# Strassen's seven products for the up and gate projections, and w2 in four parts

## The chip, the cores and the metric

The kernel runs on one core of one Trainium2 chip. Five engines work side by side, each with its own queue of instructions, and wait for each other through semaphores: TensorE (PE; its weight loads are shown apart as PEld), VectorE (DVE), ScalarE (ACT), GpSimd (POOL) and SyncE (SP, which only issues transfers). The metric is the device time of one execution in microseconds (us). One execution before was also recorded by the hardware profiler; its rows are what follows is read from.

## The reference

The model is a trunk of two layers over 512 tokens of width 1024. Each layer is a feed-forward sublayer (FFN), a mixer of three branches, and a second FFN; every sublayer is modulated by a conditioning vector and closed by a layer norm. All is float32. The FFN is what the change touches:

```
def swiglu(h, w1, w3, w2):
    return (jax.nn.silu(h @ w1) * (h @ w3)) @ w2

f = swiglu(modulate(h, shift, scale), w1, w3, w2)     # w1, w3: 1024 x 2816, w2: 2816 x 1024
h = layer_norm(alpha * h + 0.5 * gate * f)
```

There are four FFNs, (0, 0), (0, 2), (1, 0) and (1, 2) as (layer, place); the mixers are (0, 1) and (1, 1).

## The kernel before

Activations lie transposed: x is 8 tiles, one for each 128 of the width, with 512 tokens in the columns. A float32 product is made of three passes (mm3, line 126): the weight and the activation are each split into a high part, rounded to the format that TensorE multiplies, and a low part, the rest; the passes are high with high, high with low, and low with high. `split` (line 132) makes both parts of an activation: the high one by ACT (line 135), the low one by DVE (line 138).

Weights come in chunks of four 128x128 tiles, 128x512 in all. `wtile` (lines 99 to 117) issues the transfer on SP, has ACT round the high part (line 109, tile whi) and DVE subtract it from the raw chunk (line 111, tile wlo). In tails, where `share` is set, POOL subtracts every other one. There are 9 buffers of whi and wlo (WBUFS).

`gemm` (line 539) multiplies a column of weight tiles with x into one PSUM bank of 512 columns and then calls `tick`, which lets one step of side work run: the conditioning's matrix (`ada_jobs`, line 207, two DVE reductions on a transferred chunk for each 128 outputs, line 185), and, under the first FFN of a layer, the tables and state-space powers of the coming mixer (lines 480 to 760; the powers are the short POOL operations of lines 529 to 537).

An FFN (`ffn_body`, line 442) goes over 22 column blocks f of 128. The first ones are made by `first_block` (line 397), three in the first FFN and two in the others, there in two halves of 256 tokens, with the steps of the previous sublayer's norm between their matmuls. For every f follow a gemm with w1, a gemm with w3, and `swiglu_out` (line 430): silu on ACT, the product on DVE, the split into the tile pair g. After 11 blocks their g is multiplied by the upper half of w2 and added, times the gate G, to the residual H (lines 470 to 473); G must be ready by then (line 468). The other 11 go through `tail` (line 372): as each of the 8 column blocks of w2 is done, the sums of the norm are formed; the last three blocks are done in halves of 256 tokens, and `norm` (line 319) of the first half runs beside the matmuls of the second. `norm` spreads mean and deviation over the partitions by a matmul (line 316), subtracts, scales, modulates (lines 345 to 364) and last scales H for the next residual on POOL (line 368).

The order of the work is that of the program, as the framework's scheduler issues it: each engine takes its instructions strictly in the order printed, and one that waits holds up those behind it.

Of the kernel before, what the change touches and what calls it, by code (L numbers as in the profile page):

```python
# [9 lines left out]
F32 = mybir.dt.float32  # L10
# [6 lines left out]
P = 128  # L17
# [18 lines left out]
WBUFS, RBUFS, ABUFS = 9, 4, 2  # L36
# [4 lines left out]
class Packer:  # L41


    def __init__(self):
        self.tiles = []
        self.ada = []


class Builder:
    def __init__(self, nc, tc, ctx, A, pk, plan):  # L50
# [11 lines left out]
        self.ntile = 0  # L62
        self.nada = 0
        self.cur = None
        self.share = False
# [33 lines left out]
    def wtile(self, key):  # L99

        i = self.ntile % CH
        if i == 0:
            nc = self.nc
            c = self.ntile // CH
            raw = self.wp.tile([P, CH * P], F32, tag="wraw", name=f"wraw{c}", bufs=RBUFS)
            nc.sync.dma_start(raw, self.A["ws"][c])
            hi = self.wp.tile([P, CH * P], F32R, tag="whi", name=f"whi{c}", bufs=WBUFS)
            lo = self.wp.tile([P, CH * P], F32R, tag="wlo", name=f"wlo{c}", bufs=WBUFS)
            nc.scalar.copy(hi, raw)  # L109
            e = nc.gpsimd if self.share and c % 2 else nc.vector  # L110
            e.tensor_tensor(lo, raw, hi.bitcast(F32), ALU.subtract)  # L111
            self.cur = (hi, lo)
        self.ntile += 1
        self.pk.tiles.append(key)
        hi, lo = self.cur
        s = slice(i * P, (i + 1) * P)
        return hi[:, s], lo[:, s]

    def wide(self, keys):

        assert self.ntile % CH == 0 and len(keys) == CH
        for key in keys:
            self.wtile(key)
        return self.cur
# [247 lines left out]
    def tail(self, keys, xs, G, nxt, last):  # L372
# [3 lines left out]
        NS = 4 if len(xs) == KT else 3  # L376
# [53 lines left out]
    def swiglu_out(self, f, g, p1, p3, a, b):  # L430
        nc = self.nc
        n = b - a
        s = self.t(self.fp, "sil", 3)
        nc.scalar.activation(s[:, :n], p1, AF.Silu)
        nc.vector.tensor_tensor(s[:, :n], s[:, :n], p3, ALU.mult)  # L435
        self.normed = self.split(s[:, :n], g[0][:, a:b], g[1][:, a:b]).ins

# [4 lines left out]
    def ffn_body(self, l, i, nxt, last, pend):  # L442
        fi = 0 if i == 0 else 1
        G = self.mod[l, i][2]
        NH = DFF // P // 2
        for hf in range(2):
            f0 = hf * NH
            g = []
            ahead = []
            if hf == 0:  # L450
                fs = range(2 if pend else 3)
                g = [self.pair(self.fp, "g", 12) for _ in fs]
                names = [lambda k, f=f, m=m: (m, (l, fi), k, f) for f in fs for m in ("ffn_w1", "ffn_w3")]
                if pend is None:
                    names.append(lambda k: ("ffn_w1", (l, fi), k, 3))
                for a, b, pp in self.first_block(names, pend):
                    ahead = pp[2 * len(fs):]
                    for f in fs:
                        self.swiglu_out(f, g[f], pp[2 * f], pp[2 * f + 1], a, b)
            for f in range(f0 + len(g), f0 + NH):  # L460
                pp, ahead = ahead, []
                for m in ("ffn_w1", "ffn_w3")[len(pp):]:
                    pp.append(self.gemm([(m, (l, fi), k, f) for k in range(KT)], self.x))
                gt = self.pair(self.fp, "g", 12)
                self.swiglu_out(f, gt, pp[0], pp[1], 0, S)
                g.append(gt)
            if hf == 0:
                while (l, i) not in self.gated:
                    self.tick()
# [1017 lines left out]
```

## Time and profile before

| | |
|---|---|
| three runs | 2890.91, 2893.56, 2895.76 us, median 2893.56 us |
| profiled execution | 2893.78 us, span of the instructions 2891.7 us |
| mean granted TensorE clock | 0.987 |
| PE busy | 2801.3 us, 14360 matmuls |
| DVE busy | 1646.4 us, 4266 instructions |
| ACT busy | 1111.9 us, 2174 instructions |
| POOL busy | 438.7 us, 685 instructions |
| chunks of weights | 916, of them 872 low parts on DVE and 44 on POOL |

Engines overlap, so their busy times don't add up. The busy time of PE is that of overlapping, pipelined matmuls; the distance from one start to the next is what one of them costs. Lines such as L111 are the kernel's lines. Names such as wlo<-wraw,whi say what was written from what.

### The profile page before, as it was taken

The page shows a single profiled execution, that of the slowest core. Times are in us where ns is not written, and L with a number is a line of the kernel's source. Part 1 is how long each engine was busy: PE and PEld are TensorE (multiplying, and loading weights), DVE is VectorE, ACT ScalarE, POOL GpSimd, SP SyncE. Part 2 cuts the span into 40 slices and gives each one's busy share as a digit, 9 for nine tenths or more (in the row PEclk, how much of TensorE's full clock was granted, in tenths as well). Part 3 has the DMA queues.
Part 4 walks back from the last instruction along what each step waited for, and adds up shares of the span by engine and source line. Part 5 has one row for each costly group of instructions (what it writes and reads, how often), then busy time and mean ns, then how long its engine had stood idle before and what let it go on. Part 6 is the DMA issues. An engine that isn't in the chain of part 4 may idle for free.

```text
span 2891.7 us, 40692 instructions
## 1 busy us (share of the span) xinstructions
PE 2801.3 (97%) x14360; PEld 2364.6 (82%) x14360; DVE 1646.4 (57%) x4266; ACT 1111.9 (38%) x2174; POOL 438.7 (15%) x685
## 2 busy tenths in 40 slices
PE   8999998999999999999999999989999999999997
PEld 6888886978888888888888888869788888888886
DVE  8755459983444465544476454699734444653334
ACT  4333344373443344223343233543643433432332
POOL 2120365000000050000411003730000000500004
PEclk9999999999999999999999999999999999999998
DMA  7545345543233324544344453446422333253331
GB/s 279 167 136 146 113 125 155 182 135 117 85 90 113 98 67 146 153 124 142 88 123 143 131 148 97 149 146 190 146 81 84 99 110 98 70 150 102 95 99 51
DMA packets 205836, 359.38 MB, mean 124 GB/s; under 512 B 23104, under 2 KB 40000, under 8 KB 205632
## 3 DMA queue, kind: packets, MB, share of 16 engines
q1 hardware_dynamic: 198864, 346.32, 40.2%
q10 hardware_dynamic: 6768, 10.47, 1.1%
q8 instruction: 112, 1.84, 0.3%
q14 instruction: 92, 0.75, 0.1%
HBM read 339.92 MB, written 16.78 MB: 123 GB/s over the span
## 4 chain that ended last, share of the span: by engine, by line
PE 82%; DVE 7%; POOL 5%; ACT 3%; DMA 2%; issue 1%; ACTq 0%; SPq 0%; DVEq 0%; POOLq 0%
PE ps L128 26%; PE ps L129 25%; PE ps L130 25%; DMA wraw<-ws 1%; PE ps L894 1%; DMA araw<-wa 1%; DVE wlo L111 1%; POOL half L533 1%; POOL half L536 1%; ACT whi L109 1%; PE ps L316 1%; PE ps L1085 1%; DVE araw L185 1%; PE ps L997 1%; PE ps L1074 0%
## 5 line engine op out<-in xcount | busy, mean ns | idle before, releaser
L109 ACT CAST whi<-wraw 128x512 fp32r<-128x512 f32 x916 | 564.7, 621 | 1320.6 <-PE ps L129 931.4
L111 DVE TENSOR_TENSOR wlo<-wraw,whi 128x512 fp32r<-128x512 f32 x872 | 609.8, 703 | 740.8 <-ACT whi L109 723.2
L128 PE MATMUL ps<-xh,whi 128*128 128x512 f32 (+1 forms) x2496 | 938.7, 379 | 15.4 <-ACT xh L135 15.4
L129 PE MATMUL ps<-xl,whi 128*128 128x512 f32 (+1 forms) x2496 | 941.4, 378 | 0.2 <-DVE xl L138 0.2
L130 PE MATMUL ps<-xh,wlo 128*128 128x512 f32 (+1 forms) x2496 | 939.5, 377 | 0.0
L128 PEld LDWEIGHTS ps<-xh,whi 128*128 128x128 f32 x2496 | 469.5, 189 | 103.0 <-ACT xh L135 18.4
L129 PEld LDWEIGHTS ps<-xl,whi 128*128 128x128 f32 x2496 | 471.1, 189 | 85.3 <-issue 1.2
L130 PEld LDWEIGHTS ps<-xh,wlo 128*128 128x128 f32 x2496 | 471.0, 189 | 85.4 <-issue 0.5
L128 PE MATMUL ps<-gh,whi 128*128 128x512 f32 (+1 forms) x836 | 303.8, 363 | 0.2 <-ACT gh L135 0.2
L129 PE MATMUL ps<-gl,whi 128*128 128x512 f32 (+1 forms) x836 | 299.4, 358 | 0.2 <-DVE gl L138 0.2
L130 PE MATMUL ps<-gh,wlo 128*128 128x512 f32 (+1 forms) x836 | 299.2, 358 | 0.0
L111 POOL TENSOR_TENSOR wlo<-wraw,whi 128x512 fp32r<-128x512 f32 x44 | 57.5, 1307 | 1159.7 <-ACT whi L109 1159.7
L128 PEld LDWEIGHTS ps<-gh,whi 128*128 128x128 f32 x836 | 160.4, 192 | 25.5 <-issue 2.5
L129 PEld LDWEIGHTS ps<-gl,whi 128*128 128x128 f32 x836 | 160.3, 192 | 25.3 <-issue 2.5
L130 PEld LDWEIGHTS ps<-gh,wlo 128*128 128x128 f32 x836 | 160.1, 191 | 22.3
L303 POOL TENSOR_TENSOR H<-H,ln 128x512 f32<-128x512 f32 x6 | 7.8, 1293 | 968.3 <-ACT ln L302 968.3
L435 DVE TENSOR_TENSOR sil<-sil,ps 128x512 f32<-128x512 f32 (+1 forms) x94 | 61.1, 652 | 117.3 <-PE ps L130 113.6
L185 DVE CUSTOM_DVE_ANT_0 araw<-araw,cond,cols 128x512 f32<-128x512 f32 x128 | 96.7, 755 | 14.8 <-DMA araw<-wa 14.8
L185 DVE CUSTOM_DVE_ANT_0 araw<-araw,cond,adac 128x512 f32<-128x512 f32 x128 | 96.2, 751 | 10.9 <-DMA araw<-wa 9.9
L286 DVE SCALAR_TENSOR_TENSOR H<-ps,G,H 128x256 f32<-128x256 f32 (+1 forms) x68 | 40.2, 592 | 82.5 <-PE ps L130 82.4
L128 PE MATMUL ps<-whi,xh 128*128 128x512 f32 x192 | 80.8, 423 | 1.3 <-DVE vst L949 1.2
L130 PE MATMUL ps<-whi,xl 128*128 128x512 f32 x192 | 77.9, 406 | 0.0
(518 smaller groups left out, 3555.3 us busy)
## 6 DMA issues: line engine op xcount, KB each, us to landing
wraw<-ws SPq DMA_DIRECT2D x916, 256.0 KB, 2.7
araw<-wa SPq DMA_DIRECT2D x256, 256.0 KB, 2.8
raw<-wa SPq DMA_DIRECT2D x16, 512.0 KB, 6.9
vd<-vst SPq DMA_DIRECT2D x24, 256.0 KB, 2.1
V<-vd SPq DMA_DIRECT2D x24, 256.0 KB, 5.5
hd<-H SPq DMA_DIRECT2D x32, 128.0 KB, 1.8
H<-hd ACTq DMA_DIRECT2D x16, 256.0 KB, 3.2
H<-xT SPq DMA_DIRECT2D x8, 256.0 KB, 7.6
```

The source lines that it names most:

```text
L109: nc.scalar.copy(hi, raw)
L111: e.tensor_tensor(lo, raw, hi.bitcast(F32), ALU.subtract)
L128: nc.tensor.matmul(ps, w[0], x[0], start=start, stop=False)
L129: nc.tensor.matmul(ps, w[0], x[1], start=False, stop=False)
L130: nc.tensor.matmul(ps, w[1], x[0], start=False, stop=stop)
L185: self.nc.vector.tensor_tensor_reduce(out=w, in0=w, in1=self.cond[:, k0:k0 + n], scale=1.0, scalar=a if k0 else self.col(("b_ada", l), q), ...
L286: nc.vector.scalar_tensor_tensor(h, ps, G[:, j:j + 1], h, ALU.mult, ALU.add)
L316: self.nc.tensor.matmul(ps, self.ones, dg, start=True, stop=True)
L435: nc.vector.tensor_tensor(s[:, :n], s[:, :n], p3, ALU.mult)
L533: tt(t, a[1], b[1], ALU.mult)
L536: tt(t, a[1], b[0], ALU.mult)
L894: nc.tensor.matmul(s, q[:, P * i:P * i + P], K[:, :w], start=True, stop=True)
```

## The change

In the products with w1 and w3, x, W and the result are taken as two by two blocks: the rows of the result are the two halves of the tokens, the inner dimension is split into even and odd 128-tiles, and the column blocks are f and f + 1. Strassen's scheme in Winograd's form makes the four blocks of the result from seven block products instead of eight, with sums of blocks of x and of W as operands. A "group" is two column blocks of w1 and of w3 together: w1's block and w3's block stand side by side, so that 7 products of 24 matmuls with 256 columns replace 96 matmuls with 512 columns.

`combine_x` forms the combinations of x once for each FFN: POOL adds high and low parts of the 8 tiles, DVE makes four combinations and three splits for each pair of tiles. `group` forms those of W by 8 POOL subtractions of raw chunks (held in 12 buffers, sraw), calls `parts` for 14 chunks, combines the seven products by 7 DVE additions, and makes g by silu on ACT, 2 multiplications on POOL and the two parts (ACT and DVE). The products with w2 go in four parts of 6, 6, 4 and 6 column blocks: the first three are added to H, the last is the tail, whose last four blocks are always done in halves. There are 8 buffers of whi and wlo. The gates' conditioning is computed one sublayer earlier, but for the first FFN, where eight steps of side work run after each group until the gate is ready. No side work runs inside a group; two steps run in each gemm with w2.

```diff
-WBUFS, RBUFS, ABUFS = 9, 4, 2
+WBUFS, RBUFS, ABUFS = 8, 4, 2
+PARTS = (6, 6, 4, 6)
+SBUFS = 12
...
+    def parts(self, raw, pool=False):
+        nc = self.nc
+        hi = self.wp.tile([P, CH * P], F32R, tag="whi", name=self.name("whi"), bufs=WBUFS)
+        lo = self.wp.tile([P, CH * P], F32R, tag="wlo", name=self.name("wlo"), bufs=WBUFS)
+        nc.scalar.copy(hi, raw)
+        e = nc.gpsimd if pool else nc.vector
+        e.tensor_tensor(lo, raw, hi.bitcast(F32), ALU.subtract)
+        return hi, lo
...
-        NS = 4 if len(xs) == KT else 3
+        NS = 4
...
+    def combine_x(self):
...
+            for t, x in ((t0, x0), (t1, x1)):
+                nc.gpsimd.tensor_tensor(t, x[0].bitcast(F32), x[1].bitcast(F32), ALU.add)
+            d = nc.vector
+            a11, a21, a12, a22 = t0[:, :H], t0[:, H:], t1[:, :H], t1[:, H:]
+            d.tensor_tensor(a22, a21, a22, ALU.add)
+            d.tensor_tensor(a21, a11, a21, ALU.subtract)
+            d.tensor_tensor(a11, a22, a11, ALU.subtract)
+            d.tensor_tensor(a12, a12, a11, ALU.subtract)
+            s41 = self.pair(self.fp, "s41", KT // 2)
+            s2 = [self.t(self.fp, z, KT // 2, H, F32R) for z in ("s2h", "s2l")]
+            self.split(a11, *s2)
+            self.split(t1, *s41)
+            self.split(a21, x0[0][:, H:], x0[1][:, H:])
...
+    def group(self, l, fi, f, B, g, after):
...
+        def product(x, w):
+            ps = self.pst()
+            for d in range(2):
+                hi, lo = self.parts(w[d])
+                for q in range(2):
+                    for s in range(2):
+                        o = P * (2 * q + s)
+                        self.mm3(ps[:, H * s:H * s + H], (hi[:, o:o + P], lo[:, o:o + P]), self.xs[2 * d + q][x],
+                                 d + q + s == 0, d + q + s == 3)
+            return ps
...
+        p1 = product("A11", B["11"])
+        for d in range(2):
+            sub(B["11"][d], B["12"][d], B["11"][d])
+        for d in range(2):
+            sub(T2[d], B["22"][d], B["11"][d])
+        nc.scalar.copy(r0, p1)
+        self.group_load(l, fi, after, N, "11")
+        p2 = product("A12", B["21"])
+        for d in range(2):
+            sub(B["12"][d], B["22"][d], B["12"][d])
+        for d in range(2):
+            sub(B["21"][d], B["21"][d], T2[d])
+        add(r1, r0, p2)
+        nc.scalar.activation(r1, r1, AF.Silu)
...
+        add(r2, r0, product("S2", T2))
+        p5 = product("S1", B["11"])
...
+        add(r3, r2, product("S3", B["12"]))
+        add(r2, r2, p5)
+        add(r0, r3, p5)
+        add(r2, r2, product("S4", B["22"]))
+        nc.gpsimd.tensor_tensor(r2, r2, r1, ALU.mult)
+        out(r2, 0)
+        p4 = product("A22", B["21"])
...
+        add(r3, r3, p4)
+        nc.scalar.activation(r3, r3, AF.Silu)
+        nc.gpsimd.tensor_tensor(r0, r0, r3, ALU.mult)
+        out(r0, 1)
...
-                for n in range(KT):
-                    ps = self.gemm([("ffn_w2", (l, fi), f0 + k, n) for k in range(NH)], g)
-                    h = self.H[n]
-                    self.nc.vector.scalar_tensor_tensor(h, ps, G[:, n:n + 1], h, ALU.mult, ALU.add)
+        self.combine_x()
+        f0 = 0
+        for n in PARTS:
+            while f < f0 + n:
+                B = self.group(l, fi, f, B, g, f + 2 if f + 2 < DFF // P else None)
+                f += 2
+                if (l, i) not in self.gated:
+                    self.tick(8)
+            if f == DFF // P:
+                break
+            while (l, i) not in self.gated:
+                self.tick()
+            for j in range(KT):
+                ps = self.gemm([("ffn_w2", (l, fi), f0 + k, j) for k in range(n)], g)
+                self.tick()
+                h = self.H[j]
+                self.nc.vector.scalar_tensor_tensor(h, ps, G[:, j:j + 1], h, ALU.mult, ALU.add)
+            f0, g = f, []
...
-                yield from self.ada_jobs(l, i, True)
+                if first:
+                    yield from self.ada_jobs(l, i, True)
                 if nxt is not None:
                     yield from self.ada_jobs(*nxt, False)
+                    yield from self.ada_jobs(*nxt, True)
```

Two places of the order are shown. The first is DVE in FFN (0, 2), where the second half of x has just been normed. Before, the last low parts of x (xl, line 138) are mixed with those of the next gemms' weights (wlo, line 111):

```order
1776 L138 TENSOR_TENSOR xl_9700<-half_10441,xh_9699 128x256
1777 L138 TENSOR_TENSOR gl_10268<-sil_10505,gh_10267 128x256
1778 L111 TENSOR_TENSOR wlo_10642<-wraw_10639,whi_10641 128x512
1779 L138 TENSOR_TENSOR xl_9702<-half_10447,xh_9701 128x256
1780 L138 TENSOR_TENSOR xl_9704<-half_10452,xh_9703 128x256
1781 L111 TENSOR_TENSOR wlo_10663<-wraw_10660,whi_10662 128x512
1782 L111 TENSOR_TENSOR wlo_10681<-wraw_10678,whi_10680 128x512
```

In the changed kernel the same engine goes from the combinations of x (lines 476 to 479, on the tiles ln and lndg that POOL's sums fill; line 152 is `split`) to the weights of the first group (line 130, from sraw):

```order
1992 L476 TENSOR_TENSOR lndg_11871<-ln_1947_11870,lndg_11871 128x256
1993 L152 TENSOR_TENSOR s41l_11861<-ln_1942_11853,s41h_11860 128x512
1994 L477 TENSOR_TENSOR ln_1947_11870<-ln_1947_11870 128x256
1995 L130 TENSOR_TENSOR wlo_11898<-sraw_11800,whi_11897 128x512
1996 L478 TENSOR_TENSOR ln_1947_11870<-lndg_11871,ln_1947_11870 128x256
1997 L152 TENSOR_TENSOR xl_10884<-ln_1947_11870,xh_10883 128x256
1998 L479 TENSOR_TENSOR lndg_11871<-lndg_11871,ln_1947_11870 128x256
1999 L152 TENSOR_TENSOR s2l_11881<-ln_1947_11870,s2h_11880 128x256
2000 L130 TENSOR_TENSOR wlo_11914<-sraw_11802,whi_11913 128x512
2001 L152 TENSOR_TENSOR s41l_11879<-lndg_11871,s41h_11878 128x512
2002 L130 TENSOR_TENSOR wlo_11940<-sraw_11804,whi_11939 128x512
```

The first low part of weights, row 1995, stands behind row 1992, which reads the last of the eight sums (lndg_11871), and the second one, row 2000, behind five more operations on that pair. On POOL the same place reads so: the last steps of the norm (line 382, L368 before), the sums (line 473), and behind them the first group's subtractions (line 527):

```order
422 L382 TENSOR_SCALAR H_10860<-H_10860,R_94 128x256
423 L382 TENSOR_SCALAR H_10861<-H_10861,R_94 128x256
424 L382 TENSOR_SCALAR H_10862<-H_10862,R_94 128x256
425 L473 TENSOR_TENSOR ln_1941_11852<-xh_10879,xl_10880 128x512
426 L473 TENSOR_TENSOR ln_1942_11853<-xh_10881,xl_10882 128x512
427 L473 TENSOR_TENSOR ln_1947_11870<-xh_10883,xl_10884 128x512
428 L473 TENSOR_TENSOR lndg_11871<-xh_10885,xl_10886 128x512
429 L527 TENSOR_TENSOR sraw_11800<-sraw_11808,sraw_11800 128x512
430 L527 TENSOR_TENSOR sq_11890<-sraw_11812,sraw_11800 128x512
431 L527 TENSOR_TENSOR sraw_11808<-sraw_11812,sraw_11808 128x512
```

Before, nothing of this FFN's matmuls came from POOL at this place; now row 428 is ahead of DVE's row 1992, and rows 429 and 430 ahead of the operands of the products S1 and S2. The second place is POOL in the first FFN, at the end of the state-space powers (lines 532 to 537). Before, the powers are followed by the tail's norm:

```order
77 L534 TENSOR_TENSOR C_2296<-C_2296,half_2297 128x64
78 L536 TENSOR_TENSOR half_2297<-ssmq_850,C_2296 128x64
79 L537 TENSOR_TENSOR C_2296<-C_2296,half_2297 128x64
80 L303 TENSOR_TENSOR H_140<-H_140,ln_223_3071 128x512
81 L291 TENSOR_TENSOR H_141<-H_141,ln_223_3071 128x512
```

Now they stand between a group's weight subtractions and its multiplications (lines 552 and 558), and the next group's subtractions come behind those (the powers' lines are 662 to 667 here):

```order
104 L666 TENSOR_TENSOR half_2383<-ssmq_1014,C_2382 128x64
105 L667 TENSOR_TENSOR C_2382<-C_2382,half_2383 128x64
106 L552 TENSOR_TENSOR ln_242_1499<-ln_242_1499,ln_241_1498 128x512
107 L558 TENSOR_TENSOR lndg_1497<-lndg_1497,ln_243_1500 128x512
108 L527 TENSOR_TENSOR sraw_1539<-sraw_1653,sraw_1539 128x512
109 L527 TENSOR_TENSOR sraw_1541<-sraw_1655,sraw_1541 128x512
110 L527 TENSOR_TENSOR sq_1774<-sraw_1763,sraw_1539 128x512
```

What moved is the work of the groups, which now stands on both sides of the 48 powers in POOL's order.

## Rows read from the trace of the kernel before

**Rows 1.** The page's part 1: busy us, share of span, instructions.

```profile
PE 2801.3 (97%) x14360; PEld 2364.6 (82%) x14360; DVE 1646.4 (57%) x4266; ACT 1111.9 (38%) x2174; POOL 438.7 (15%) x685
```

**Rows 2.** Stretches: us, PE, PEld, DVE, ACT, POOL busy, clock, DMA, GB/s.

```profile
80.00:140.00 60.00, 60.00 (x266) 49.72 (x265) 40.79 (x133) 20.27 (x35) 6.71 (x14) 1.00 0.54 156
1120.00:1180.00 60.00, 60.00 (x266) 49.69 (x266) 28.16 (x53) 19.77 (x33) 0.00 (x0) 1.00 0.51 149
1430.00:1445.00 15.00, 11.37 (x70) 10.14 (x69) 11.27 (x33) 7.82 (x18) 9.27 (x11) 0.77 0.33 82
```

**Rows 3.** Timeline of PE at 120 us: start, us, what.

```profile
119.63 0.39 PE L130 MATMUL ps<-xh,wlo 128*128 128x512 f32 x1
...
122.35 0.39 PE L130 MATMUL ps<-xh,wlo 128*128 128x512 f32 x1
```

**Rows 4.** Timeline of PE near 1467 us, 256 columns.

```profile
1464.91 0.28 PE L128 MATMUL ps<-xh,whi 128*128 128x256 f32 x1
...
1469.47 0.28 PE L130 MATMUL ps<-xh,wlo 128*128 128x256 f32 x1
```

**Rows 5.** Waits of PE: us in total, times, longest.

```profile
PE ps L316 <- DVE lndg L312: 21.0, 9, 3.6
PE ps L128 <- ACT xh L135: 15.4, 8, 3.1
```

**Rows 6.** Timeline of DVE near 58 us, back to back.

```profile
58.35 0.68 DVE L486 SCALAR_TENSOR_TENSOR rt<-rt,rt 128x512 f32<-128x512 f32 x1
58.95 0.68 DVE L435 TENSOR_TENSOR sil<-sil,ps 128x512 f32<-128x512 f32 x1
```

**Rows 7.** Timelines of DVE and POOL near 342 and 334 us.

```profile
342.39 1.83 DVE L111 TENSOR_TENSOR wlo<-wraw,whi 128x512 fp32r<-128x512 f32 x1 [3.96 <-ACT whi L109]
...
342.38 1.31 POOL L111 TENSOR_TENSOR wlo<-wraw,whi 128x512 fp32r<-128x512 f32 x1
...
334.10 0.72 DVE L111 TENSOR_TENSOR wlo<-wraw,whi 128x512 fp32r<-128x512 f32 x1 [4.54 <-ACT whi L109]
...
334.23 1.74 POOL L295 TENSOR_TENSOR ln<-ln,sq 128x512 f32<-128x512 f32 x1
335.93 1.29 POOL L111 TENSOR_TENSOR wlo<-wraw,whi 128x512 fp32r<-128x512 f32 x1
```

**Rows 8.** Groups by line and form: busy us, mean ns, idle before.

```profile
L111 DVE TENSOR_TENSOR wlo<-wraw,whi 128x512 fp32r<-128x512 f32 x872 | 609.8, 703 | 740.8 <-ACT whi L109 723.2 <-PE ps L129 16.2 <-PE ps L130 0.5
L185 DVE CUSTOM_DVE_ANT_0 araw<-araw,cond,cols 128x512 f32<-128x512 f32 x128 | 96.7, 755 | 14.8 <-DMA araw<-wa 14.8
...
L435 DVE TENSOR_TENSOR sil<-sil,ps 128x512 f32<-128x512 f32 x82 | 56.3, 687 | 114.2 <-PE ps L130 113.6 <-ACT sil L434 0.7
...
L111 POOL TENSOR_TENSOR wlo<-wraw,whi 128x512 fp32r<-128x512 f32 x44 | 57.5, 1307 | 1159.7 <-ACT whi L109 1159.7
...
L109 ACT CAST whi<-wraw 128x512 fp32r<-128x512 f32 x916 | 564.7, 621 | 1320.6 <-PE ps L129 931.4 <-issue 184.4 <-DMA wraw<-ws 73.6
L434 ACT ACTIVATE sil<-ps 128x512 f32<-128x512 f32 x82 | 48.6, 593 | 1.4 <-PE ps L130 1.4
```

**Rows 9.** Timeline of POOL at the start of FFN (0, 2).

```profile
1462.72 2.53 POOL L368 TENSOR_SCALAR H<-H,R 128x256 f32<-128x256 f32 x2 [0.51 <-ACT half L363]
```

**Rows 10.** Timeline of POOL, first and last of the powers.

```profile
146.85 0.29 POOL L533 TENSOR_TENSOR half<-ssmq,half 128x64 f32<-128x64 f32 x1 [1.47 <-DVE ssmq L603]
...
163.10 0.32 POOL L537 TENSOR_TENSOR C<-C,half 128x64 f32<-128x64 f32 x1
```

**Rows 11.** The page's part 6: transfers, KB, us to landing.

```profile
wraw<-ws SPq DMA_DIRECT2D x916, 256.0 KB, 2.7
```

More of the change, by code (lines that the diff above doesn't have):

```diff
@@ L44, in __init__ @@
     def __init__(self):
-        self.tiles = []
+        self.chunks = []
         self.ada = []
@@ L99, in wtile, with chunk @@
     def wtile(self, key):
[L101 to L104, printed above, removed]
+        if self.part == CH:
+            c = len(self.pk.chunks)
             raw = self.wp.tile([P, CH * P], F32, tag="wraw", name=f"wraw{c}", bufs=RBUFS)
[L106 to L114, printed above, removed]
+            self.here = self.chunk(raw, [])
+            self.cur = self.parts(raw, self.share and c % 2)
+            self.part = 0
+        self.here.append(key)
         hi, lo = self.cur
-        s = slice(i * P, (i + 1) * P)
+        s = slice(self.part * P, (self.part + 1) * P)
+        self.part += 1
         return hi[:, s], lo[:, s]
+    def chunk(self, raw, keys):
+        self.nc.sync.dma_start(raw, self.A["ws"][len(self.pk.chunks)])
+        self.pk.chunks.append(keys)
+        return keys
+    def parts(self, raw, pool=False):
[6 more added lines that the diff above has]
+        return hi, lo
     def wide(self, keys):
-        assert self.ntile % CH == 0 and len(keys) == CH
+        assert self.part == CH and len(keys) == CH
         for key in keys:
@@ new lines, in ffn_body @@
+        g = []
+        fs = range(2 if pend else 3)
+        for _ in range(0, len(fs), 2):
+            self.g_pair(g)
+        names = [lambda k, f=f, m=m: (m, (l, fi), k, f) for f in fs for m in ("ffn_w1", "ffn_w3")]
+        if pend is None:
+            names.append(lambda k: ("ffn_w1", (l, fi), k, 3))
+        for a, b, pp in self.first_block(names, pend):
+            for f in fs:
+                self.swiglu_out(g[f], pp[2 * f], pp[2 * f + 1], a, b)
+        if pend is None:
+            p3 = self.gemm([("ffn_w3", (l, fi), k, 3) for k in range(KT)], self.x)
+            self.swiglu_out(g[3], pp[6], p3, 0, S)
@@ L474, in ffn_body @@
         self.tick(99)
[L475 removed]
+        return self.tail(lambda j: [("ffn_w2", (l, fi), f0 + k, j) for k in range(len(g))], g, G, nxt, last)
     def sincos(self, eng, b, s, c, t, u):
@@ L1420, in host_ssm, with host_weights @@
     return lam, bc.reshape(DEPTH, 4, P, 256)
[L1423 removed]
+def host_weights(I, chunks, n):
     out = np.zeros((n, P, CH, P), np.float32)
[L1425 to L1431 removed]
+    for c, tiles in enumerate(chunks):
+        for t, (name, idx, k, cols) in enumerate(tiles):
+            w = I[name]
+            for q in idx:
+                w = w[q]
+            if isinstance(cols, (int, np.integer)):
+                cols = slice(cols * P, (cols + 1) * P)
+            out[c, :, t, :] = w[k * P:(k + 1) * P, cols]
     return out.reshape(n, P, CH * P)
@@ L1473 @@
         Builder(nc, tc, ctx, A, pk, plan).run()
-    assert -(-len(pk.tiles) // CH) == nch and len(pk.ada) == nada, (len(pk.tiles), nch, len(pk.ada), nada)
-    arrays["ws"] = host_weights(I, pk.tiles, nch)
+    assert len(pk.chunks) == nch and len(pk.ada) == nada, (len(pk.chunks), nch, len(pk.ada), nada)
+    arrays["ws"] = host_weights(I, pk.chunks, nch)
     arrays["wa"] = host_ada(I, pk.ada)
```

87 lines of the change are left out of this document (48 added, 39 removed).

## The prediction

> **What bounds the kernel now.** The page's table of engines comes first: TensorE (PE) is busy 97% of the span of 2891.7 us, VectorE (DVE) 57%, GpSimd (POOL) 15% [rows 1]. Then the stretches: in a settled part of a feed-forward sublayer (FFN) PE is busy 60.00 of 60.00 us and DVE 28.16; in the first FFN, which also carries the conditioning and the mixer's tables, DVE is busy 40.79; at the seam between two sublayers PE gets 11.37 of 15 and its granted clock is 0.77 [rows 2]. PE's own rows give the prices: twelve 512-column matmuls in 2.72 us, 0.2267 us each [rows 3], and 38 steps of 256 columns in 4.56 us, 0.120 us each [rows 4]. The waits of PE are few: 21.0 us for nine norms' spreading and 15.4 us for eight first inputs [rows 5]. So a step that is saved on PE is saved in full, if the other engines hand it operands as fast as before. That is the whole question.
>
> **What goes.** A group is two column blocks of w1 and w3. Before: 4 gemms of 8 k tiles by 3 passes, 96 x 0.2267 = 21.76 us. After: 7 products of 24 matmuls, 168 x 0.120 = 20.16. That is 1.60 us, not the eighth that the count suggests, because 256 columns cost more than half of 512 (0.120 against 0.113). 39 groups (9 in the first FFN, 10 in each other): -62 us. The tails go in 256-wide halves over 24 tiles instead of 33, a further -1.
>
> The Trainium skill, "TensorE: Matmul & The Clock Gate", section "Back-to-back issue gap", gives an isolated gap of N/2.4 + 2.5 ns, that is 215.8 and 109.2; as an estimate by it the groups would save 39 x (20.72 - 18.35) = 92 us. The rows say 0.2267 and 0.120 [rows 3, 4], and they decide.
>
> **What comes: DVE and POOL in a group.** For its 14 operand chunks (8 before) a group needs 14 low-part subtractions on DVE, 7 additions with a product in PSUM, 2 low parts of g; POOL gets 8 weight subtractions and 2 multiplications, all of 512 columns. By themselves these fit: DVE 23 x 0.60 us (its spacing back to back [rows 6]) = 13.8, POOL 10 x 1.29 = 12.9 [rows 7], ScalarE 14 casts of 0.62 [rows 8] and five more, about 12, against 20.16 of PE. But they don't run beside each other. In the trace a DVE subtraction that starts with a POOL one at 342.38 takes 1.83 us, where the mean of all is 0.70 [rows 8], ending 0.53 after POOL's; where DVE's began first, POOL's took 1.74 instead of 1.29 [rows 7]. So an operation with two inputs in SBUF on DVE and one on POOL go in turn. The additions have one input in PSUM and stay out of it (that is an inference from rows of L435, whose mean of 687 ns shows no such lengthening [rows 8]). The turn-taking load of a group is 10 x 1.29 + 16 x 0.57 = 22.0 us, more than PE's 20.16. Besides, DVE's low part of g waits for POOL's multiplication, in POOL's order this stands behind the next group's subtractions, and behind the waiting DVE instruction are queued the low parts that PE needs next; an estimate of 3 us for that makes a cycle of about 25 us. Four products of lookahead (8 weight buffers) hide most in parts of two or three groups, and the gemms with w2 between the parts let both engines catch up: I take 3.6 us for each part of three groups and nothing for one of two, 3 x 11 + 8 = +41 us. Bounds: 0, if the lookahead hides all, and 39 x (25 - 20.16) = 189 if it hides none.
>
> The Trainium skill, "SBUF — State Buffer", section "Who interferes with whom", says that a DVE instruction with two SBUF inputs contends with GpSimd reads through a shared interface, one with at most one SBUF input does not. The trace agrees (1.83 for 0.70 us). By it DVE and POOL add up as above; without it they would fit beside each other and this term were 0.
>
> **The start of FFNs two to four.** The first block ends at 1469.6 [rows 4], and before, the next gemm's weights were ready. Now x must be recombined: POOL rebuilds 8 tiles from hi and lo (8 x 1.29 = 10.3 us) in the order between its norm operations, which end at 1465.25 even now [rows 9]; so its last sum comes at about 1475. DVE takes that sum in order ahead of the second weight chunk of the first product (order of DVE shown with the change), with four combinations and three splits per pair of tiles. Without its low parts PE can issue four matmuls. I get a wait of 8.2 us for the first product; then POOL's weight subtractions stand behind the sums, eight in turn with DVE's low parts, and the products S2, S1, S3 come 4.4, 2.3 and 1.2 us late. 16 us, three times: +48 (bounds 7 and 20 each: 7 where only the last sum is late).
>
> **The first FFN.** Three pieces. The recombination: 8 x 1.29 on POOL and 28 narrow operations on DVE (about 10 us), against one gemm of 5.44 us that covers it; DVE is loaded there already (40.79 of 60 [rows 2]): +10. Second, the gate G must be ready before w2's part 0 can leave PSUM, and DVE has 16 conditioning reductions at 0.75 (12.1 us [rows 8]), 13 low parts at 0.60 (7.8 [rows 6]) and some 65 operations of the tables ahead of it, about 17 of them 512 wide at 0.60 (10.2), the rest narrower (an estimate of 8), 37 to 39 us in all, against 6 x 3 x 8 x 0.2267 = 32.6 us of PE: after eight banks PE stops, about 6 us, and the low parts of the next group, queued among the same operations, come late by some 11 more: +17. Third, POOL's chain of state-space powers (48 operations, 44 of them from 146.85 to 163.42, 16.6 us [rows 10]) stand in its order between the subtractions of two groups, where before no PE work stood behind them: +10 after lookahead. Together +37, bounds 12 and 55.
>
> **Small ones.** w2 now starts 16 times instead of 8: 13 matmuls of cover (2.95 us) against addition, silu, multiplication, cast (0.69 + 0.59 + 1.29 + 0.62 and hand-over, 3.6): 0.65 us, in the four short parts (4 k tiles, 7 matmuls) 2.0: +16. Tails have 24 matmul groups instead of 33 to cover the norm: three seams, +7. The granted clock is 0.77 in the 15 us of the seam where PE stands still for 3.6 [rows 2], which is 2.6 us of work lost to it (11.37 x 0.23); for waits of 8 us and more at four places or so I add +9. DMA moves 234 more chunks of 256 KB, at a DMA share of about half [rows 2]: nothing, since each is issued a group ahead and lands in 2.7 us [rows 11]; SP's queue holds the chunks of w2 behind those of the next group, which wait for one of 12 buffers, and if that cover were gone one landing, 2.7 us, would show per part. The gates' conditioning comes one sublayer earlier, under gemms that leave DVE idle half the time [rows 2], and the eighth instead of the ninth weight buffer is counted in the lookahead.
>
> **Sum.** -62 - 1 + 41 + 48 + 37 + 16 + 7 + 9 = +95 against the profiled run's own 2893.78 us (span 2891.7; the median of the three runs, 2893.56, is the same to 0.01%): about 2988 us.
>
> **Rivals.** (a) *The saved steps come through.* The lookahead hides DVE and POOL, each seam costs some 3 us, the first FFN 12, w2's starts 8: -63 + 9 + 12 + 8 = -34, about 2860; with nothing lost at all 2831. For it: DVE idles half the time in settled parts [rows 2]. Against: a load in turn of 22.0 us against 20.16, and an order that puts the low parts behind POOL's sums. (b) *Only the seams cost.* The groups run at PE's pace, the rest as summed: 2988 - 41 = 2947. (c) *DVE and POOL in turn pace every group* at 24 us or more; it decides from 21.76 on, where a group is no shorter than before: 39 x (24 - 21.76) = +87, and 37, 24 (part of the seams is then hidden behind the same queue), 16, 7, 9 and the tails' -1: +179, 3073. For it: every operation that POOL is given reads two inputs in SBUF. (d) *Gains and waits cancel*, within 6 us of before. That the change doesn't halve its columns or drop a product is excluded: the order of PE has 168 matmuls of 256 in a group.
>
> **Chances.** My forecast (2965 to 3030) 0.48, (b) 0.24, (c) 0.11, (a) 0.13, (d) 0.04. Bounds: (a) and a part of (d) lie below 2890, about 1 in 7, the worst of (c) above 3072, about 1 in 20; so 2890 to 3072. 0.2% (about what a measurement of this kernel tells from no change) are 5.8 us. Faster 0.13, same 0.04, slower 0.83.
>
> **What would show it.** After: matmuls of w1 and w3 at 0.120 us; PE waits on DVE's low parts (wlo) of 8 us at 1470 and the like; DVE's low parts with a mean clearly above 703 ns and POOL's subtractions above 1307; POOL busy some 33% of the span (438.7 + 39 x 12.9 + 32 x 1.29 = 983 us). If PE shows 60 of 60 us in stretches of three groups, the 41 us were wrong; if the first product at each seam waits under 3 us, the 48; if DVE's mean stays at 0.70 us, the turn-taking, and rival (a) stands.

## The result and the profile after

The changed kernel takes 3219.49 us (median of 4 runs, 3217.15 to 3222.82) against 2893.26 us: the ratio is 1.1128, 95% interval 1.1109 to 1.1148. It is slower, as forecast, but by 326 us and not by 95, and so outside the range. Sixteen runs of the kernel before spread from 2890.59 to 2898.42 us; each experiment below is one run unless more are named, so differences of less than some 8 us between two of them are not told apart. The page after has, where [rows 1] stood before:

```profile
PE 2851.7 (89%) x17060; PEld 2519.9 (78%) x17060; DVE 2211.4 (69%) x4903; ACT 1276.0 (40%) x2499; POOL 1062.0 (33%) x1091
```

PE stands idle for 3217.5 - 2851.7 = 365.8 us of the span, before for 90.4: that is 275 of the 326 us. The other 50 are busy time, though the groups need 62 us fewer of it: matmuls run longer, because the granted clock of the whole execution fell from 0.987 to 0.942. The waits of PE, in total, times and longest, answer to [rows 5]:

```profile
PE ps L142 <- ACT gh L523: 99.3, 16, 8.0
PE ps L144 <- DVE wlo L130: 73.3, 37, 12.3
PE ps L142 <- ACT whi L128: 56.1, 23, 9.4
PE ps L330 <- DVE lndg L326: 25.4, 7, 4.0
```

The first line is new and the largest: each of the 16 parts of w2 waits some 6 us for the high part of g. Lines by form, of DVE and then of POOL (busy us, mean ns, idle before), answer to [rows 8]:

```profile
L130 DVE TENSOR_TENSOR wlo<-sraw,whi 128x512 fp32r<-128x512 f32 x468 | 407.0, 885 | 79.9 <-ACT whi L128 79.2 <-POOL C L667 0.7
L130 DVE TENSOR_TENSOR wlo<-wraw,whi 128x512 fp32r<-128x512 f32 x564 | 406.6, 731 | 325.8 <-ACT whi L128 314.4 <-PE ps L143 8.1 <-DMA wraw<-ws 2.0
L528 DVE TENSOR_TENSOR ln<-ln,ps 128x512 f32<-128x512 f32 x156 | 105.7, 678 | 0.9 <-PE ps L144 0.8
...
L527 POOL TENSOR_TENSOR sraw<-sraw,sraw 128x512 f32<-128x512 f32 x156 | 250.4, 1614 | 406.1 <-DVE wlo L130 355.1 <-DMA sraw<-ws 19.5 <-DVE half L642 16.3
```

Low parts of the groups take 885 ns instead of 703, POOL's subtractions 1614 instead of 1307, while DVE's additions with a product in PSUM keep 678. Both engines lengthen each other, and only where DVE too reads two inputs in SBUF: 93 additions with a product in PSUM that ran beside a POOL operation of 512 columns took 689 ns at most.

Stretches of FFN (0, 2), as in [rows 2]: w2's first part, three groups, w2's second part, the tail.

```profile
1269.20:1311.40 42.20, 34.33 (x146) 27.99 (x145) 33.55 (x56) 10.99 (x18) 15.44 (x10) 0.92 0.51 156
1311.40:1376.80 65.40, 62.41 (x505) 61.86 (x505) 48.55 (x67) 29.08 (x51) 30.51 (x20) 0.97 0.36 109
1376.80:1419.30 42.50, 35.75 (x147) 28.95 (x146) 34.43 (x57) 11.05 (x19) 16.13 (x10) 0.88 0.52 158
1562.70:1618.10 55.40, 42.89 (x230) 37.41 (x229) 32.05 (x70) 18.09 (x35) 27.22 (x22) 0.88 0.33 101
```

Three groups need 3 x 20.16 = 60.5 us and take 65.4; a part of w2 with 144 matmuls needs 32.6 and takes 42. So here the groups run nearly at PE's pace, and w2 behind them pays. Counted like this (length less matmuls by 0.2267 or 0.120 us) for all four FFNs, in us lost; "first parts" are the stretches ahead of the first w2, "groups later" those between parts of w2:

| kernel | time | first parts | w2's starts | groups later | tails |
|---|---|---|---|---|---|
| before | 2893 | 18 | 1 | 0 | 30 |
| changed | 3219 | 107 | 120 | 121 | 83 |
| sums on POOL, not used | 3192 | 113 | 138 | 69 | 86 |
| multiplications on DVE | 3140 | 104 | 81 | 77 | 86 |
| no sums | 2990 | 75 | 38 | 27 | 58 |
| all sums on DVE | 3009 | 90 | 17 | 55 | 56 |
| the same, x not combined | 2942 | 23 | 16 | 55 | 57 |
| part 0 plain, all on DVE | 2943 | 44 | 6 | 38 | 56 |
| four parts, plain gemms | 2923 | 23 | 2 | 0 | 51 |

From the first row to the second the losses grow by 89 + 119 + 121 + 53 = 382 us; less 63 us of saved steps, and with some 7 in the mixers, that is the 326.

### The profile page after: what moved, and what is told of

The parts are those of the page before. It is cut to its first block, busy times and chain, and to the rows that moved or that the text cites. A ratio compares the mean times of both kernels' runs of the same rounds, so it can differ in the third digit from the quotient of the medians.

```text
span 3217.5 us, 48169 instructions
## 1 busy us (share of the span) xinstructions
PE 2851.7 (89%) x17060; PEld 2519.9 (78%) x17060; DVE 2211.4 (69%) x4903; ACT 1276.0 (40%) x2499; POOL 1062.0 (33%) x1091
## 5 line engine op out<-in xcount | busy, mean ns | idle before, releaser
L144 PE MATMUL ps<-xh,wlo 128*128 128x256 f32 (+1 forms) x2496 | 823.6, 331 | 45.0 <-DVE wlo L130 44.9
L142 PE MATMUL ps<-xh,whi 128*128 128x256 f32 (+1 forms) x2496 | 817.9, 331 | 37.8 <-ACT xh L149 20.0
L143 PE MATMUL ps<-xl,whi 128*128 128x256 f32 (+1 forms) x2496 | 823.1, 330 | 3.1 <-DVE xl L152 2.7
L128 ACT CAST whi<-wraw 128x512 fp32r<-128x512 f32 x604 | 367.0, 619 | 696.7 <-PE ps L143 382.0
L130 DVE TENSOR_TENSOR wlo<-wraw,whi 128x512 fp32r<-128x512 f32 x564 | 406.6, 731 | 325.8 <-ACT whi L128 314.4
L130 DVE TENSOR_TENSOR wlo<-sraw,whi 128x512 fp32r<-128x512 f32 x468 | 407.0, 885 | 79.9 <-ACT whi L128 79.2
L142 PE MATMUL ps<-gh,whi 128*128 128x512 f32 (+1 forms) x800 | 312.2, 391 | 99.3 <-ACT gh L523 99.3
L527 POOL TENSOR_TENSOR sraw<-sraw,sraw 128x512 f32<-128x512 f32 x156 | 250.4, 1614 | 406.1 <-DVE wlo L130 355.1
L128 ACT CAST whi<-sraw 128x512 fp32r<-128x512 f32 x468 | 276.3, 617 | 229.6 <-PE ps L143 221.9
L142 PE MATMUL ps<-s41h,whi 128*128 128x256 f32 x624 | 183.5, 294 | 43.3 <-ACT whi L128 43.3
L144 PE MATMUL ps<-s41h,wlo 128*128 128x256 f32 x624 | 186.3, 299 | 24.6 <-DVE wlo L130 24.4
```

The lines of the kernel that those rows point to most:

```text
L142: nc.tensor.matmul(ps, w[0], x[0], start=start, stop=False)
L143: nc.tensor.matmul(ps, w[0], x[1], start=False, stop=False)
L144: nc.tensor.matmul(ps, w[1], x[0], start=False, stop=stop)
L527: sub = lambda o, x, y: nc.gpsimd.tensor_tensor(o, x, y, ALU.subtract)
```

## The experiments

**Parts alone.** `for n in PARTS` goes around the plain gemms of before, with the changed kernel's tails and its earlier conditioning:

```diff
+        for part, n in enumerate(PARTS):
...
+            for f in range(f0 + len(g), f0 + n):
...
                 for m in ("ffn_w1", "ffn_w3")[len(pp):]:
                     pp.append(self.gemm([(m, (l, fi), k, f) for k in range(KT)], self.x))
```

> The kernel before with the products with w2 in the four parts of 6, 6, 4 and 6 column blocks, the last four blocks of the tail in halves and the gates' conditioning one sublayer earlier, but with plain 512-column gemms for w1 and w3. Theory (the waits come with the seven products: long chains through DVE, POOL and ACT ahead of the last g): here the last g is only a silu, a multiplication and a cast away (about 1.9 us), which the 13 matmuls of the other column blocks cover; the short parts cost 1 us each and the tails some 10 together: 2900 to 2915 us. Rival (four parts cost what they do whatever makes g): the 12 starts of w2 that lose some 9.5 us each and the tails that lose 53 us stay: about 3055 us.

It took 2922.6 us at a granted clock of 0.983, beside 2895.9: some 8 us over the forecast's range and far from the rival. Starts of w2 cost nothing; 21 of the 27 us are in the tails. So four parts by themselves are cheap, and the 119 us at w2's starts come with the products.

**Without the weight sums.**

```diff
-            sub(B["11"][d], B["12"][d], B["11"][d])
...
-            sub(T2[d], B["22"][d], B["11"][d])
+        T2 = B["12"]
...
-            sub(B["12"][d], B["22"][d], B["12"][d])
...
-            sub(B["21"][d], B["21"][d], T2[d])
```

> The changed kernel without the 8 weight subtractions of each group; the products take raw chunks in place of the sums, so the result is not the reference's. Theory of turns (DVE and POOL in turn pace the groups): DVE's low parts of the groups come back from 885 ns to about 700, the parts of three groups lose 30 instead of 110 us, the first parts 12 instead of 22 each, 3219 - 80 - 40 = about 3100 us. Rival (the order of DVE's queue, not the turns): the starts of w2, 99 us of waits, stay and the parts of three groups keep most of their loss: 3170 to 3200 us.

It took 2990.3 us: 229 us come back, about twice what the theory of turns asked for, and w2's starts fall from 120 to 38. The rival is out, since those starts were what it said would stay. But the run takes away the wait for the sums along with POOL's load.

**Sums that nobody uses.** POOL's eight subtractions stay, into scratch, and the products take the raw chunks:

```diff
-            sub(B["11"][d], B["12"][d], B["11"][d])
+            sub(T2[d], B["12"][d], B["11"][d])
...
-        add(r2, r0, product("S2", T2))
+        add(r2, r0, product("S2", B["12"]))
```

> The changed kernel in which POOL makes 8 sums of weight chunks per group as before, but into scratch that nothing reads; the products take raw chunks, so the result is not the reference's. POOL's load and its turns with DVE stay, the wait for the sums goes. It stands against the run without the sums (2990 us). Theory (turns): DVE's low parts of the groups keep a mean near 885 ns and most of the 229 us stays: 3130 us or more. Rival (ACT and DVE wait for POOL's sums, the turns matter little): low parts near 700 ns in effect on PE nothing, about 2990 to 3020 us.

It took 3192.0 us, with low parts at 1059 ns:

```profile
L130 DVE TENSOR_TENSOR wlo<-sraw,whi 128x512 fp32r<-128x512 f32 x546 | 566.6, 1059 | 62.5 <-ACT whi L128 60.4
```

202 of the 229 us are back though nothing waits for a sum: POOL's work beside DVE is enough. It is not the changed kernel's own mix, though. There low parts lengthen less (885 ns), and DVE also stands idle (the third figure) for what POOL has still to deliver, through ACT; the first two rows are the changed kernel's, the last two those of the next run:

```profile
L524 DVE TENSOR_TENSOR gl<-ln,gh 128x512 fp32r<-128x512 f32 x39 | 26.9, 690 | 78.7 <-ACT gh L523 77.3
L130 DVE TENSOR_TENSOR wlo<-sq,whi 128x512 fp32r<-128x512 f32 x78 | 71.7, 922 | 62.0 <-ACT whi L128 62.0
...
L524 DVE TENSOR_TENSOR gl<-ln,gh 128x512 fp32r<-128x512 f32 x39 | 26.7, 686 | 15.0 <-ACT gh L523 15.0
L130 DVE TENSOR_TENSOR wlo<-sq,whi 128x512 fp32r<-128x512 f32 x78 | 51.4, 682 | 3.7 <-ACT whi L128 3.7
```

How the cost divides between lengthened operations and such waits is not shown.

**All sums on DVE.**

```diff
-        sub = lambda o, x, y: nc.gpsimd.tensor_tensor(o, x, y, ALU.subtract)
+        sub = lambda o, x, y: nc.vector.tensor_tensor(o, x, y, ALU.subtract)
...
-        nc.gpsimd.tensor_tensor(r2, r2, r1, ALU.mult)
+        nc.vector.tensor_tensor(r2, r2, r1, ALU.mult)
...
-        nc.gpsimd.tensor_tensor(r0, r0, r3, ALU.mult)
+        nc.vector.tensor_tensor(r0, r0, r3, ALU.mult)
```

> The changed kernel with the 8 weight subtractions and the 2 multiplications of each group on DVE instead of POOL. DVE then has 33 operations of 0.60 us, 19.8 of PE's 20.16 us in a group, and no turns with POOL. Theory of turns: the load in turn was 22.0 us and more, so the groups get faster, 3120 to 3180 us, and the chain to g shortens by 2 x 0.7 us at the start of w2. Rival (DVE's queue is the bound): the low parts now stand behind 10 more operations, every part of three groups loses more: 3230 to 3300 us.

It took 3009.3 us: 210 us less with the same arithmetic, by giving the busier engine ten operations more per group, and over 110 us below the range that was expected. Three groups and the w2 behind them in FFN (0, 2), as above:

```profile
1246.10:1306.60 60.50, 60.50 (x506) 60.48 (x505) 54.48 (x88) 33.40 (x55) 0.00 (x0) 1.00 0.41 131
1306.60:1339.60 33.00, 33.00 (x147) 26.87 (x146) 30.09 (x62) 8.61 (x14) 0.00 (x0) 1.00 0.56 173
```

PE is busy without a gap at a granted clock of 1.00, and DVE is busy 54.48 of 60.50 us, 18.2 us a group; its low parts take 688 ns. The gain of 1.60 us per group is there, in this stretch.

**Only the multiplications on DVE** (the last two replacements of that diff).

> The changed kernel with only the 2 multiplications of each group on DVE; the 8 weight subtractions stay on POOL. Moving all ten gave 3009 us. Theory (turns over the whole group): POOL's load falls from 12.9 to 10.3 us, DVE's rises by 1.2, the load in turn from 22.0 to 20.6, still over 20.16: a part comes back, 3120 to 3170 us. Rival (the multiplications in POOL's order hold up g, and with it the starts of w2): nearly all comes back, about 3030 us; if they don't matter, 3200 us or more.

It took 3140.5 us, inside the range of the turns. The two multiplications were 79 us of the 210, and w2's starts fall from 120 to 81.

**Filling the waits.** 28 matmuls into an unused bank ahead of each part of w2:

```diff
+        warm = self.pst()
+        for _ in range(28):
+            self.nc.tensor.matmul(warm, self.xs[0]["A11"][0][:, :P], self.x[0][0], start=True, stop=True)
...
+            self.fill(g)
```

> The changed kernel with 28 matmuls of 512 columns that nothing uses (28 x 0.2267 = 6.35 us) ahead of each of the 16 parts of w2, where PE waits 99 us in all. Theory (the clock falls because PE stands still): the waits are filled, the granted clock stays at 1.0 through the starts of w2, and the about 3.4 us of work lost to half clock there come back: 16 x 3 = 48 us, about 3170 us. Rival (the clock falls for another reason, or the dummies only push the work back): the clock is as before in those places and the time 3210 to 3260 us.

It took 3204.6 us: 15 us less, between theory and rival and close to the rival. The losses of w2's parts and of the tails fall by 112 us, and the fillers take 16 x 6.35 = 102. Of the 112, 86 are the wait for g itself, which falls from 99.3 to 13.1 us. So the waiting was most of the cost; the half clock behind it can have been worth some 26 us at most at these places, not 48.

**x not combined**, on top of all sums on DVE: the products take blocks of x in place of s2, s41 and S3.

```diff
...
-            self.split(a11, *s2)
-            self.split(t1, *s41)
-            self.split(a21, x0[0][:, H:], x0[1][:, H:])
...
-                            "S2": tuple(s2), "S3": half(x0, 1), "S4": half(s41, 0)})
+                            "S2": half(x1, 0), "S3": half(x0, 1), "S4": half(x0, 0)})
```

> The run with all sums of a group on DVE (3009 us), without the combinations of x: the products take blocks of x itself, so the result is not the reference's. Theory (recombining x holds up the first group of each FFN): the first parts lose 5 us as before instead of about 24 in three FFNs, and the first FFN some 15 less: 3009 - 57 - 15 = about 2937 us. Rival (the first group is held up by its weights and the norm, not by x): 2985 to 3005 us.

It took 2941.7 us, within 5 of the forecast: the recombination costs 68 us there, all in the first parts (90 to 23).

**Part 0 plain**, x recombined under it, groups from part 1 on, all sums on DVE.

```diff
...
+                while f < n:
+                    self.g_pair(g)
+                    for _ in range(2):
+                        pp = [self.gemm([(m, (l, fi), k, f) for k in range(KT)], self.x) for m in ("ffn_w1", "ffn_w3")]
+                        self.swiglu_out(g[f], *pp, 0, S)
+                        f += 1
+                        late = late or self.combine_x()
```

> All sums of a group on DVE, and the first part of each FFN with plain gemms; the combinations of x are made under these, and the groups begin with the second part. 7 of 39 groups are lost (+11 us). Theory: the first parts of three FFNs lose 6 instead of 24 us (-54), the first FFN's first two stretches some 20 less, and DVE's side work finds more gemms to run under: 3009 + 11 - 54 - 20 = about 2945 us. Rival (the work only moves on, and the second part waits instead): 3000 us or more.

It took 2942.6 us, as the theory said. What is left over before is one stretch of FFN (0, 0) that loses 28 us under the mixer's side work, 26 us each in the first parts and in the tails, and some smaller losses, against a gain of 51 from 32 groups.

**Idle POOL work in the kernel before**, 4 or 7 subtractions per column block:

```diff
+        if n == S:
+            w = self.t(self.fp, "turn")
+            for q in range(4):
+                nc.gpsimd.tensor_tensor(w, w if q else s, self.x[q][0].bitcast(F32), ALU.subtract)
```

> The kernel before, with 4 idle POOL subtractions of 512 columns (a chain whose first reads the tile sil) behind each of the 82 column blocks that are made in full width. Per block of 10.88 us of PE: POOL 4 x 1.29 = 5.2, DVE's operations with two SBUF inputs 5 x 0.57 = 2.9, side work up to 1.3, 9.3 us in turn. Theory (turns cost only where their sum passes PE's time): 2893 to 2905 us. Rival (every lengthened low part delays PE): 82 blocks by some 2 us, 3000 us and more.

> The same with 7 idle POOL subtractions per block: 9.0 + 2.9 = 11.9 us in turn, 13.2 with side work, more than PE's 10.88, though POOL by itself (9.0) and DVE by itself have time left. Theory (turns): every half of 11 blocks runs 1.0 to 2.3 us per block too long, less what three buffers absorb: 2920 to 3020 us. Rival (POOL and DVE run beside each other, and what cost time in the changed kernel was its order): 2893 to 2905 us, as with 4.

They took 2930.9 and 3046.1 us beside 2896.6, both some 26 us over the range expected. With 4, FFNs (0, 2) and (1, 2) lose next to nothing (under 3 us more than before), as forecast; the 34 us are all in (0, 0) and (1, 0), under which the state-space powers of POOL and DVE's tables run too, which the expectation left out. With 7 the cost is 150 us, and 137 of it are in these two FFNs again; (0, 2) loses 10 more than before and (1, 2) 4. So a load in turn just above PE's time costs little by itself in 11 blocks, and much where side work comes on top; that it is the side work was not tried by itself. Low parts take 917 ns with 7:

```profile
L111 DVE TENSOR_TENSOR wlo<-wraw,whi 128x512 fp32r<-128x512 f32 x872 | 788.0, 917 | 488.2 <-ACT whi L109 469.4 <-PE ps L129 14.2 <-DMA V<-vd 2.0
```

FFN (1, 0), the gemms of the first half and the w2 behind them:

```profile
1532.20:1661.10 128.90, 124.31 (x635) 105.25 (x635) 116.73 (x206) 46.35 (x92) 86.99 (x69) 1.00 0.36 106
1661.10:1754.90 93.80, 64.49 (x266) 51.12 (x265) 63.63 (x156) 20.96 (x39) 42.68 (x65) 0.84 0.38 116
```

The gemms, which need 121.0 us, lose 8; the gemms with w2, which need 59.8, lose 34, and in 24.3 of these PE waits for the high part of g. No Strassen is in this kernel, and nothing needs the idle sums; only the buffers that they read stay held for them. The delay builds up where POOL and DVE overlap and is paid where the last g is needed.

**Groups only where they are cheap.** FFN (0, 0), or (0, 0) and (1, 0), as before in halves of 11; in the others groups from the second part on (8 each), all sums on DVE, x recombined under w2's first part, tails with five blocks in halves.

```diff
+        plain = (l, i) in PLAIN
+        parts = (11, 11) if plain else PARTS
...
+                if not plain and not part and j == 0:
+                    B = {}
+                    for kind in ("11", "21", "12", "22"):
+                        self.group_load(l, fi, f, B, kind)
+                    self.combine_x()
...
-        steps = [len(xs) + k for k in NORM_STEPS]
+        steps = [(STEP6 if len(xs) == 6 else len(xs)) + k for k in NORM_STEPS]
```

> Groups only where they are cheap: in FFNs (0, 2), (1, 0) and (1, 2), from the second part on (24 groups, all sums on DVE); the first part plain, x recombined under the first part of w2; FFN (0, 0) wholly as before, in halves of 11. The tail of 6 column blocks has five instead of four blocks in halves and the norm's steps after 11 and 21 tiles. Gain 24 x 1.6 = 38 us. Theory: the first parts lose nothing more, FFN (1, 0)'s second part 8 us for the mixer's side work, the tails 3 to 7 each: -38 + 8 + 15 = 2871 to 2885 us. Rival (x's recombination holds up w2 or the groups wherever it stands): 2900 us or more.

> The same with FFN (1, 0) as before too: 16 groups, gain 26 us, the tails of two FFNs 3 to 7 each: 2877 to 2885 us. If the side work of the mixer in (1, 0) costs more than 12.8 us in the other run, this one is the faster of the two; if less, the slower.

> The kernel with groups in FFNs (0, 2) and (1, 2) from the second part on, all sums on DVE, x recombined under w2's first part, and FFNs (0, 0) and (1, 0) as before; one look gave 2884.1 us beside 2896.6 for the kernel before. Theory (its segments lose 8.6 and 5.4 us against a gain of 12.8 each, and (0, 0)'s tail loses 2.4 less): ratio 0.995 to 0.9965, an interval clear of 1. Rival (a single look): within 0.2% of before.

> The same kernel with the tails of 6 column blocks as in the changed kernel: four blocks in halves instead of five, the norm's steps after 6 and 16 matmul groups instead of 11 and 21. Two FFNs have such a tail. Theory (the first norm is asked for before its sums are ready, and fewer matmuls stand beside it): 2 to 4 us more per tail, 4 to 8 us slower than with five blocks. Rival (the tail loses what the chain of the norm takes, however the blocks are cut): within 2 us of it.

With three FFNs it took 2901.6 us, worse than forecast and in the rival's range. The rival's cause is not there, though: w2's first part, under which x is recombined, loses 1.0 us in each of the three. FFN (1, 0) under the mixer's side work loses more than it gains: it is 8 us longer than in the run with two. The rest of the 17 us between the two runs is in the mixer behind it (689 to 680 us) and was not followed up. With two FFNs it took 2884.1 in a single run and a median of 2882.07 in five more (2878.62 to 2882.74): the ratio to before is 0.9952, interval 0.994 to 0.9964. This version beats both kernels, before by half a per cent. Its page:

```profile
PE 2780.8 (97%) x15494; PEld 2401.2 (83%) x15494; DVE 1911.1 (66%) x4718; ACT 1190.2 (41%) x2314; POOL 438.3 (15%) x689
```

With four blocks in the tails it took 2888.09 us (median of 11), ratio 0.9977, interval 0.9968 to 0.9986: 3 us more per short tail, as the theory had it.

## Why the prediction was right and wrong

**Right: the price of the steps.** The prices were 0.2267 and 0.120 us, and 1.60 us saved per group: with the sums on DVE three groups take 60.50 us.

**Right: the mechanism.** DVE and POOL take turns, additions from PSUM stay outside them, and the cycle is longer than PE's. The forecast had about 25 us for it. In FFN (0, 2) POOL begins the third group's subtractions 25.8 us after the second's, and the same distance of 25.7 to 25.8 us is found in seven of the eight parts of three groups behind a first w2:

```profile
1323.08 1.30 POOL L527 TENSOR_TENSOR sraw<-sraw,sraw 128x512 f32<-128x512 f32 x1 [14.12 <-DVE wlo L130]
1348.89 1.67 POOL L527 TENSOR_TENSOR sraw<-sraw,sraw 128x512 f32<-128x512 f32 x1 [7.68 <-DVE wlo L130]
...
1323.08:1348.89 25.81, 25.81 (x218) 25.81 (x217) 18.57 (x24) 12.43 (x22) 15.25 (x11) 1.00 0.25 72
```

For 22.1 of the 25.81 us POOL or a DVE operation with two inputs in SBUF is running (counted from the trace's records), where the load in turn was put at 22.0; in the other 3.7 neither is. The 0.57 us for one DVE operation in that load stands in no row; with 0.53 [rows 7] or 0.60 [rows 6] it is 21.4 or 22.5. PE is busy all through this stretch: the lateness is there and does not show yet.

**Wrong: what the turns cost.** The term was 41 us; moving all ten operations off POOL measured 210, more than the term's upper bound. The step that failed is the sentence "Four products of lookahead hide most in parts of two or three groups, and the gemms with w2 between the parts let both engines catch up". With a cycle of 25 us, the step before it, and nothing hidden the term was 189, a bound that was then set aside for a fifth of it; with the measured 25.8 it is 39 x (25.8 - 20.16) = 220. The lookahead hides lateness from the products but doesn't remove it. In FFNs (0, 2) and (1, 2), which carry no work for a mixer, the later parts of three groups lose 5 to 12 us where 3.6 were taken, and each w2 behind a part loses 8 to 10 where 0.65 to 2.0 were. DVE in the changed kernel at the second start of w2 (start, us, what, what it waited for):

```profile
1378.84 0.69 DVE L130 TENSOR_TENSOR wlo<-wraw,whi 128x512 fp32r<-128x512 f32 x1 [0.63 <-ACT whi L128]
1379.45 0.68 DVE L528 TENSOR_TENSOR ln<-ln,ps 128x512 f32<-128x512 f32 x1
1380.18 2.36 DVE L130 TENSOR_TENSOR wlo<-wraw,whi 128x512 fp32r<-128x512 f32 x2
1382.68 0.69 DVE L524 TENSOR_TENSOR gl<-ln,gh 128x512 fp32r<-128x512 f32 x1
1383.29 0.68 DVE L528 TENSOR_TENSOR ln<-ln,ps 128x512 f32<-128x512 f32 x1
...
1386.71 0.69 DVE L524 TENSOR_TENSOR gl<-lndg,gh 128x512 fp32r<-128x512 f32 x1 [2.15 <-ACT gh L523]
```

POOL and PE beside it:

```profile
1380.30 1.70 POOL L552 TENSOR_TENSOR ln<-ln,ln 128x512 f32<-128x512 f32 x1 [13.29 <-ACT whi L128]
1384.77 1.26 POOL L558 TENSOR_TENSOR lndg<-lndg,ln 128x512 f32<-128x512 f32 x1 [2.78 <-ACT ln L557]
```

```profile
1386.73 0.79 PE L142 MATMUL ps<-gh,whi 128*128 128x512 f32 x1 [6.75 <-ACT gh L523]
```

PE's last product ended at 1376.8. The last additions stand in DVE's queue behind low parts, one chain after the other: 1379.45 for the first half of g, and 1383.29, behind gl, for the second. POOL meets DVE's low parts once more (1.70 and 2.36 us). The 13 matmuls of cover were right, but the chain took 9.9 us from PE's end and not 3.6. With all sums on DVE the same work loses 0.4 us there, so the forecast's 16 us for w2's starts mistook the chain for the cause: it is the backlog in front of it. POOL is idle for 13.29 us before its first row here; the bill comes when the engine that made it has stopped.

The Trainium skill, "Perfetto Trace Analysis", section "Optimizing Scalar/DVE Operations", warns that moving work between DVE and GpSimd may not help, as they share a read port. The run with all sums on DVE agrees: ten operations per group cost 210 us more on POOL than on DVE.

**Nearly right: x's recombination.** It was put at 48 us for three seams and 10 for the first FFN, and 68 were measured, with the sums on DVE; in the changed kernel itself it was not taken out alone. The first low part at 1220.68 kept PE waiting for 11.91 us where 8.2 were forecast:

```profile
1220.68 0.58 PE L144 MATMUL ps<-xh,wlo 128*128 128x256 f32 x1 [11.91 <-DVE wlo L130]
```

The step left out a second wait: eight sums go through four tiles, so POOL also waits for DVE's splits.

```profile
1208.55 5.35 POOL L473 TENSOR_TENSOR ln<-xh,xl 128x512 f32<-128x512 f32 x3 [2.43 <-DVE s2l L152]
1214.87 1.26 POOL L473 TENSOR_TENSOR lndg<-xh,xl 128x512 f32<-128x512 f32 x1 [0.96 <-DVE s41l L152]
1220.71 4.81 POOL L527 TENSOR_TENSOR sraw<-sraw,sraw 128x512 f32<-128x512 f32 x1 [4.58 <-DVE wlo L130]
```

**Too small: side work.** G and the powers were given 27 us in FFN (0, 0). With the turns gone w2's first part and the three groups after it still lose 11 + 32, and FFN (1, 0), which was given nothing, 13 and 9 in its groups. No tick runs inside a group, so the side work crowds into w2; that this, and not the amount of it, is the cause was not tried by itself.

**Too small: the tails, +7.** Parts alone show +21 of the 53, and moving POOL's work to DVE takes back 27.

**Too small: the clock, +9.** PE is busy 50 us more for 63 us less of steps. In all-on-DVE it is busy 62 us less than in the changed kernel: the low clock goes where the waits go. A stretch right behind the wait of 6.75 us above reads 0.50 after, the lower of the clock's two levels (1.2 of 2.4 GHz):

```profile
1384.00:1392.00 8.00, 5.27 (x12) 4.12 (x13) 3.96 (x8) 2.32 (x4) 1.26 (x1) 0.50 0.46 154
```

**Without effect: the transfers.** The forecast had 234 more chunks to move and counted them as nothing. They were not there: the sums are made on the chip, and the changed kernel moves 604 and 312 chunks, 916 as before [rows 11].

**The rivals.** The nearest was (c), the turns that pace every group, given 0.11 and 3073 us; it had the mechanism but still a cycle of 24, halved seams and no backlog. The signs given beforehand held: low parts and POOL's subtractions lengthened, the first product at a seam waited over 8 us, POOL was busy 33%.

## What to carry to other kernels

Add up the time of two engines that take turns before comparing it with the engine that bounds; where the sum is larger, giving the work back to the busier of the two can be much faster (210 us here). Lookahead is a loan: if the cycle is too long, look for the place where the consumer needs the last result, and count the delay there. A saving of 7% per group (1.60 of 21.76 us) was worth its side costs only in stretches that had no other work to displace; the fastest version here keeps 16 of the 39 groups.

## What the runs showed of the hardware

Turns are not fair. POOL's subtraction at 1220.71, shown above, took 4.81 us, while DVE ran its short operations without a gap; these are its rows in that time:

```profile
1220.55 0.42 DVE L478 TENSOR_TENSOR ln<-lndg,ln 128x256 f32<-128x256 f32 x1
1220.88 0.42 DVE L152 TENSOR_TENSOR xl<-ln,xh 128x256 fp32r<-128x256 f32 x1
...
1222.49 0.69 DVE L152 TENSOR_TENSOR s41l<-lndg,s41h 128x512 fp32r<-128x512 f32 x1
1223.09 1.30 DVE L130 TENSOR_TENSOR wlo<-sraw,whi 128x512 fp32r<-128x512 f32 x2
```

Three more of POOL's operations in this trace took 3.9 to 4.8 us in the same way. A DVE subtraction of 512 columns that met one of POOL's TENSOR_TENSOR operations waited for the rest of that one operation: it took 1.83 us in [rows 7], and 1.79 at most in the changed kernel. So here DVE, with many short operations in a row, held POOL off for several of them, and POOL held DVE off for one.
